# A two-layer encoder on one core: weight differences placed later in the queues, and block products in twos and threes behind every second up tile

## The chip, the cores and the metric

The kernel runs on one core of a Trainium2 chip. The metric is the device time of one execution in microseconds (us); lower is better. PE is the matrix engine (PEld its weight loads), DVE the vector engine, ACT the scalar engine, POOL and SP two further engines; here SP only issues the transfers of weights.

## The reference

Two layers, each an attention and Fourier mixer followed by a convolutional feed-forward block, on 272 tokens (16 of them dropped at the end) of 2048 channels. The change concerns the feed-forward block (D_FF = 5632):

```python
h2 = _rmsnorm(h_stream, norm_ffn[i])
up = h2 @ w_up[i]
u_gate = _dwconv3_centred(up[..., :D_FF], w_conv[i], b_conv[i])
u_val = up[..., D_FF:]
h_stream = h_stream + (jax.nn.silu(u_gate) * u_val) @ w_down[i]
```

All data are float32.

## The kernel before

**Chunks.** Every weight matrix is cut into chunks of 128 x 1024 float32 values (512 KB; four tiles of 128 rows by 256 columns). `order` lists all products of the kernel with their chunks, in the order in which PE takes them; `group` walks that list. A chunk passes through three engines: SP loads it into one of four `raw` buffers (`load_raw`), ACT rounds it to a high half `wh` (L230), DVE subtracts that from `raw` to get a low half `wl` (L233). `wh` and `wl` have three buffers each. `advance` and `pump` issue the halves two chunks ahead of the one that PE works on. PE multiplies high by high, high by low and low by high part of the data: for a gate group (`ug`, 258 or 272 columns wide) 24 matmuls per chunk (L304 to L306). In layer 1 a value group (`uv`) has both data parts side by side and takes 16 matmuls per chunk, 8 of them 512 wide (L300, L301).

**The up tiles.** Gate group `ug` i (4 chunks) and value group `uv` i (4 chunks) give 256 hidden channels. After a gate group comes its evacuation: for each half of 128 channels `u` (DVE, L1105), `cv` (ACT, L1107), two convolution steps on `cv` (DVE, L1109 and L1110), silu (ACT, L1111) and a product with `rstdB` (DVE, L1112).

**The block products.** The first 32 of the 44 tiles of the hidden channels of layer 1 do not go through an ordinary `w_down` product. They are taken in pairs of tiles, and seven products of blocks (`PRODUCTS`) replace eight; the data side of each is a combination `sx`, rounded to `cb` (L1017, L1018), and the weight side is a block of `w_down` or a difference of blocks. There are two sets of 16 tiles, so two sets of 7 x 8 = 56 products. Each is one chunk with 6 matmuls of 512 columns on PE (`block_`, L1046, `ps_x`); `gather` adds the result of 8 of them to `C4` (L1030). The first set is mixed into the 64 up chunks of the second 16 tiles, the second set into the 48 up chunks of the last 12. Where a product goes is decided in the loop around L170: `at` counts up chunks, `done` the products placed.

**The weight differences.** The four differences that each of the 16 pairs (`q`) needs are made during the feed-forward block of layer 0 by `weight_sums`, a generator that `step` advances (one call after every two of a chunk's eight pairs of tile and half, so four calls per up or down chunk). A block is loaded into `b0` to `b3` by a transfer that ACT issues (L977). Ahead of it ACT copies one column of the current `wh` into the buffer (L976), which ties the transfer to that place. DVE subtracts (L980), and ACT issues the store to `ts` in device memory (L982). The numbers in `yield 9` are calls of `step` until the generator goes on.

**What sets the order.** Each engine takes its queue in order. The framework's scheduler arranges the queue from the order of the code, the dependencies and its own estimates; buffers are reused when their last reader is through.

Of the kernel before, what the change touches and what calls it, by code (L numbers as in the profile page):

```python
# [10 lines left out]
F32 = mybir.dt.float32  # L11
F32R = mybir.dt.float32r
AF = mybir.ActivationFunctionType
ALU = mybir.AluOpType
AX = mybir.AxisListType

P = 128
D = 2048
# [17 lines left out]
NPR = sum(FF_SPLIT[-1][:2]) // 2  # L36
# [84 lines left out]
def encoder_kernel(ctx, tc, xT, params, consts, bmat, w_in, w_abr, w_four, w_f64, w_out, w_up, w_down, w_blk, outT):  # L121
    nc = tc.nc
    dram = ctx.enter_context(tc.tile_pool(name="dram", bufs=1, space=bass.MemoryType.DRAM))
    tsum = [[dram.tile([P, D // 2], F32, name=f"ts{q}_{e}") for e in range(4)] for q in range(NPR)]
# [7 lines left out]
    for l in range(DEPTH):  # L132
        def g(w, mg, k0, k1):
            return [(w[l, mg, c], CW) for c in range(k0 // CW, k1 // CW)]
        if l == 0:
            f01 = [g(w_in, IN_F + i, 0, KT) for i in range(2)]
            order.append(((l, "f01"), [ch for pr in zip(*f01) for ch in pr]))
        for i in range(2 if l == 0 else 0, 4):
            order.append(((l, "f", i), g(w_in, IN_F + i, 0, KT)))
        order.append(((l, "k", 0), g(w_in, IN_K, 0, KT)))  # L140
        order.append(((l, "v", 0), g(w_in, IN_V, 0, KT)))
        for i in range(4):
            order.append(((l, "q", i), g(w_in, IN_Q + i, 0, KT)))
        for half in range(2):
            for kind, j in BRANCH_ORDER[half]:
                w, off, n = {"ga": (w_in, IN_GA, KT), "gf": (w_in, IN_GF, KT), "s": (w_four, 0, 8), "a": (w_abr, 0, 8)}[kind]
                order.append(((l, kind, j), g(w, off + j, 0, n)))
            for mg in range(8):
                order.append(((l, "o", half, mg), g(w_out, mg, 8 * half, 8 * half + 8)))
        k0 = 0  # L150
        for c, n in enumerate(FF_SPLIT[l]):
            ups = []
            for i in range(k0 // MG, (k0 + n) // MG):
                ups.append(((l, "ug", i), g(w_up, i, 0, KT)))
                ups.append(((l, "uv", i), g(w_up, FT // MG + i, 0, KT)))
            if l == DEPTH - 1 and c:
                xs_, q0 = [], (k0 - FF_SPLIT[l][c - 1]) // 2
                for p, _ in PRODUCTS:
                    for q in range(FF_SPLIT[l][c - 1] // 2):
                        src = {1: w_blk[2 * (q0 + q), 0], 2: w_blk[2 * (q0 + q) + 1, 0], 3: w_blk[2 * (q0 + q) + 1, 1],  # L160
                               5: tsum[q0 + q][0], 7: tsum[q0 + q][1], 6: tsum[q0 + q][2], 4: tsum[q0 + q][3]}[p]
                        xs_.append((src.rearrange("p (c m) -> p c m", c=CW), (c - 1, p, q)))
                slots = sum(len(chs) for _, chs in ups)
                at = done = 0
                for u, (key, chs) in enumerate(ups):
                    mixed = []
                    for ch in chs:
                        mixed.append(ch)
                        at += 1
                        while done < len(xs_) and done * slots < at * len(xs_):  # L170
                            mixed.append(xs_[done])
                            done += 1
                    ups[u] = (key, mixed)
                assert done == len(xs_)
            order += ups
            if l < DEPTH - 1 or c == len(FF_SPLIT[l]) - 1:
                for mg in range(8):
                    order.append(((l, "d", c, mg), g(w_down, mg, k0, k0 + n)))
            k0 += n
# [3 lines left out]
    st = {"raw": 0, "fetch": 0, "next": 0, "grp": 0}  # L183
# [13 lines left out]
    def advance(upto):  # L197
        while st["raw"] < min(upto + RAW, len(chunks)):
            load_raw(st["raw"])
            st["raw"] += 1  # L200
        while st["fetch"] < min(upto, len(chunks)):
            i = st["fetch"]
            if i in folded:
                todo.append((i, lambda i=i: fold_w(i)))
            todo.append((i, lambda i=i: split_w(i, 0, CW)))
            st["fetch"] += 1
# [14 lines left out]
    def split_w(i, a, b, eng=None):  # L221
        if i not in splits:
            h = wp.tile([P, CW, MG * P], F32R, tag="wh", name=f"wh{i}")
            lo = wp.tile([P, CW * MG * P + 64], F32R, tag="wl", name=f"wl{i}")
            o = wl_at[i]
            splits[i] = h, lo[:, o:o + CW * MG * P].rearrange("p (c m) -> p c m", c=CW)
        h, lo = splits[i]
        r = raws[i]
        if eng is None:
            nc.scalar.copy(h[:, a:b], r[:, a:b])  # L230
        else:
            eng.tensor_copy(h[:, a:b], r[:, a:b])
        nc.vector.tensor_tensor(lo[:, a:b], r[:, a:b], h[:, a:b].bitcast(F32), op=ALU.subtract)  # L233
        if b == CW:
            del raws[i]
# [112 lines left out]
    def first_groups(pss):  # L348
# [17 lines left out]
        for i, c0, c1, ks in ((0, 0, 1, (0,)), (0, 1, 2, (1,)), (1, 0, 2, ()), (0, 2, 4, (2, 3)), (1, 2, 4, ())):  # L366
            for k in ks:
                norm_split(k, P_NM)
            split_w(i, c0, c1, nc.vector if (i, c0) == (0, 0) else None)
# [56 lines left out]
    small = ctx.enter_context(tc.tile_pool(name="small", bufs=4))  # L426
# [92 lines left out]
    for l in range(DEPTH):  # L519
# [7 lines left out]
        with tc.tile_pool(name=f"mix{l}", bufs=1) as mp:  # L527
# [394 lines left out]
            for half in range(2):  # L922
                mH = mL = None
                for kind, i in BRANCH_ORDER[half]:
# [19 lines left out]
                    else:  # L944
# [6 lines left out]
                        for m in range(MG):  # L951
                            k = 2 * j + m
                            t_, h_ = tha[i][:, m, lo:T], mH[:, k, lo:T]
# [13 lines left out]
        with tc.tile_pool(name=f"ffn{l}", bufs=1) as fp:  # L967
# [2 lines left out]

            def weight_sums():
                tt = nc.vector.tensor_tensor
                for q in range(NPR):
                    b = [fp.tile([P, D // 2], F32, tag=f"b{e}", name=f"b{e}") for e in range(4)]
                    for e, sums in ((0, ()), (1, ((0, 1, 0, 0),)), (3, ((1, 3, 1, 1), (3, 3, 0, 2))), (2, ((2, 2, 3, 3),))):
                        nc.scalar.copy(b[e][:, 0:1], st["cur"][:, 0, 0:1].bitcast(F32))  # L976
                        nc.scalar.dma_start(b[e], w_blk[2 * q + e // 2, e % 2])  # L977
                        yield 9
                        for o, x, y, to in sums:
                            tt(b[o], b[x], b[y], op=ALU.subtract)  # L980
                            yield 2
                            nc.scalar.dma_start(tsum[q][to], b[o])  # L982
                        yield 3

            sets, prods = [], {"have": {}}
            if last:
# [79 lines left out]
            if l == DEPTH - 2:  # L1066
                behindhand.append([24, weight_sums()])
# [142 lines left out]
```

## Time and profile before

| | |
|---|---|
| runs, median (lowest to highest of 3) | 2525.16 us (2524.92 to 2531.62) |
| the profiled execution's own time | 2528.11 us |
| its span, first to last instruction | 2526.0 us |
| mean granted PE clock | 0.999 |
| PE / PEld / DVE / ACT busy | 2511.2 / 2441.2 / 1852.2 / 1276.4 us |
| DMA | 557.63 MB, 221 GB/s on average |

The span is divided as follows: layer 0 up to about 530 us its mixer, 530 to 1230 its feed-forward block, and layer 1 after that; the block products run from about 1980 to 2450 us. The busy time of a matmul in the trace is longer than the distance to the next one, because matmuls overlap; the distance from one start to the next is read from the timeline.

### The profile page before, as it was taken

To read this page: it belongs to the slowest core of one execution; us is meant where nothing else is said; L and a number is where in the kernel's file an instruction comes from. 1 tells how busy PE (TensorE), PEld (TensorE's weight loads), DVE (VectorE), ACT (ScalarE), POOL (GpSimd) and SP (SyncE) were. 2 spreads that over 40 slices of the span, in tenths; PEclk is the share of its full clock that TensorE was granted. 3 is DMA by queue.
4 is the path that set the end of the run, shared out by engine and by line. 5 is a ranking of instruction groups with operands and counts; after the bars stand their busy time and mean duration, and the time that the engine had idled before them with its cause. 6 is when DMAs were issued, how large, how long until landed. Compare 5 with 4: busy or idle time off the path is not lost.

```text
span 2526.0 us, 47879 instructions
## 1 busy us (share of the span) xinstructions
PE 2511.2 (99%) x19404; PEld 2441.2 (97%) x19404; DVE 1852.2 (73%) x2851; ACT 1276.4 (51%) x1857; POOL 18.3 (1%) x37
## 2 busy tenths in 40 slices
PE   9999999999999999999999999999999999999999
PEld 9999999999999999999999999999999989988888
DVE  7687867776776556676556887677766788879985
ACT  6455544554444334444444564445644565556653
POOL 0000000000000000000000000000000000000000
PEclk9999999999999999999999999999999999999999
DMA  7545666568888887787554555666656677778875
GB/s 240 166 157 161 194 185 190 189 225 283 286 282 281 277 292 266 270 288 266 183 179 151 175 157 188 196 201 200 188 189 192 217 243 247 244 249 256 260 244 174
DMA packets 157501, 557.63 MB, mean 221 GB/s; under 512 B 18144, under 2 KB 22112, under 8 KB 157280
## 3 DMA queue, kind: packets, MB, share of 16 engines
q1 hardware_dynamic: 134480, 482.54, 59.5%
q10 hardware_dynamic: 22800, 72.04, 8.1%
q8 instruction: 152, 2.49, 0.4%
q14 instruction: 69, 0.57, 0.1%
HBM read 516.07 MB, written 35.65 MB: 218 GB/s over the span
## 4 chain that ended last, share of the span: by engine, by line
PE 95%; DVE 2%; DMA 1%; ACT 1%; issue 1%; ACTq 0%; SPq 0%; DVEq 0%
PE ps_ug L306 6%; PE ps_ug L304 6%; PE ps_uv L300 6%; PE ps_ug L305 6%; PE ps_x L1046 6%; PE ps_d L306 4%; PE ps_d L304 4%; PE ps_d L305 4%; PE ps_uv L301 3%; PE ps_uv L306 3%; PE ps_uv L304 3%; PE ps_uv L305 3%; PE ps_o L304 2%; PE ps_o L306 2%; PE ps_o L305 2%; PE ps_gf L304 2%
## 5 line engine op out<-in xcount | busy, mean ns | idle before, releaser
L233 DVE TENSOR_TENSOR wl<-raw,wh 128x1024 fp32r<-128x1024 f32 (+1 forms) x883 | 1073.8, 1220 | 442.5 <-ACT wh L230 438.2
L230 ACT CAST wh<-raw 128x1024 fp32r<-128x1024 f32 (+1 forms) x882 | 920.9, 1046 | 853.6 <-PE ps_ug L305 171.4
L306 PE MATMUL ps_ug<-xHL,wl 128*128 128x272 f32 (+1 forms) x1408 | 397.6, 282 | 2.7 <-DVE wl L233 2.7
L304 PE MATMUL ps_ug<-xHL,wh 128*128 128x272 f32 (+1 forms) x1408 | 399.1, 283 | 0.0
L305 PE MATMUL ps_ug<-xHL,wh 128*128 128x272 f32 (+1 forms) x1408 | 397.1, 282 | 0.0
L306 PEld LDWEIGHTS ps_ug<-xHL,wl 128*128 128x128 f32 x1408 | 264.5, 188 | 3.1 <-DVE wl L233 3.1
L305 PEld LDWEIGHTS ps_ug<-xHL,wh 128*128 128x128 f32 x1408 | 264.8, 188 | 2.2
L304 PEld LDWEIGHTS ps_ug<-xHL,wh 128*128 128x128 f32 x1408 | 264.3, 188 | 2.7
L300 PE MATMUL ps_uv<-xHL,wh 128*128 128x512 f32 x704 | 247.7, 392 | 0.0
L306 PE MATMUL ps_d<-gHL,wl 128*128 128x272 f32 (+1 forms) x728 | 208.3, 286 | 2.5 <-DVE wl L233 2.5
L304 PE MATMUL ps_d<-gHL,wh 128*128 128x272 f32 (+1 forms) x728 | 208.8, 287 | 0.0
L305 PE MATMUL ps_d<-gHL,wh 128*128 128x272 f32 (+1 forms) x728 | 207.4, 285 | 0.0
L304 PE MATMUL ps_uv<-xHL,wh 128*128 128x272 f32 x704 | 201.3, 286 | 0.0
L306 PE MATMUL ps_uv<-xHL,wl 128*128 128x272 f32 x704 | 200.7, 285 | 0.0
L305 PE MATMUL ps_uv<-xHL,wh 128*128 128x272 f32 x704 | 199.9, 284 | 0.0
L301 PE MATMUL ps_uv<-xHL,wl 128*128 128x256 f32 x704 | 198.3, 282 | 0.0
L300 PEld LDWEIGHTS ps_uv<-xHL,wh 128*128 128x128 f32 x704 | 132.0, 188 | 28.6
L1046 PE MATMUL ps_x<-wh,cb 128*128 128x512 f32 x448 | 156.6, 393 | 0.0
L304 PE MATMUL ps_ga<-xHL,wh 128*128 128x272 f32 (+1 forms) x512 | 147.0, 287 | 0.0
L304 PE MATMUL ps_gf<-xHL,wh 128*128 128x272 f32 (+1 forms) x512 | 145.8, 285 | 0.1
L304 PE MATMUL ps_o<-mH,wh 128*128 128x272 f32 (+1 forms) x512 | 144.6, 282 | 0.0
L306 PE MATMUL ps_ga<-xHL,wl 128*128 128x272 f32 (+1 forms) x512 | 144.6, 282 | 0.0
(306 smaller groups left out, 5979.8 us busy)
## 6 DMA issues: line engine op xcount, KB each, us to landing
raw<-in_w_up SPq DMA_DIRECT2D x352, 512.0 KB, 4.4
raw<-in_w_in SPq DMA_DIRECT2D x206, 512.0 KB, 3.6
raw<-in_w_down SPq DMA_DIRECT2D x112, 512.0 KB, 4.3
raw<-in_w_out SPq DMA_DIRECT2D x64, 512.0 KB, 3.9
b<-in_w_blk ACTq DMA_DIRECT2D x64, 512.0 KB, 5.0
ts<-b ACTq DMA_DIRECT2D x64, 512.0 KB, 3.6
raw<-ts SPq DMA_DIRECT2D x64, 512.0 KB, 4.5
raw<-in_w_blk SPq DMA_DIRECT2D x48, 512.0 KB, 4.4
```

Source lines behind the costliest of these rows:

```text
L230: nc.scalar.copy(h[:, a:b], r[:, a:b])
L233: nc.vector.tensor_tensor(lo[:, a:b], r[:, a:b], h[:, a:b].bitcast(F32), op=ALU.subtract)
L300: nc.tensor.matmul(o2, h[:, c, sl], ab, start=kt == 0, stop=False)
L301: nc.tensor.matmul(o, lo[:, c, sl], ab[:, 0, :], start=False, stop=kt == nk - 1)
L304: nc.tensor.matmul(o, h[:, c, sl], a, start=kt == 0, stop=False)
L305: nc.tensor.matmul(o, h[:, c, sl], b, start=False, stop=False)
L306: nc.tensor.matmul(o, lo[:, c, sl], a, start=False, stop=kt == nk - 1)
L1046: nc.tensor.matmul(ps[e], cb[:, s_, q - q4], w, start=q == 0 and a == 0, stop=q == n - 1 and a == 2)
```

## The change

```diff
-                        while done < len(xs_) and done * slots < at * len(xs_):
+                        while done < len(xs_) and at % 2 == 0 and done * slots < at * len(xs_):
...
             o = wl_at[i]
+            st["new"] = h
...
             def weight_sums():
                 tt = nc.vector.tensor_tensor
-                for q in range(NPR):
-                    b = [fp.tile([P, D // 2], F32, tag=f"b{e}", name=f"b{e}") for e in range(4)]
+                b, due = {}, []
+                for q in range(NPR + 1):
                     for e, sums in ((0, ()), (1, ((0, 1, 0, 0),)), (3, ((1, 3, 1, 1), (3, 3, 0, 2))), (2, ((2, 2, 3, 3),))):
-                        nc.scalar.copy(b[e][:, 0:1], st["cur"][:, 0, 0:1].bitcast(F32))
-                        nc.scalar.dma_start(b[e], w_blk[2 * q + e // 2, e % 2])
-                        yield 9
-                        for o, x, y, to in sums:
-                            tt(b[o], b[x], b[y], op=ALU.subtract)
-                            yield 2
-                            nc.scalar.dma_start(tsum[q][to], b[o])
-                        yield 3
+                        if q < NPR:
+                            t_ = fp.tile([P, D // 2], F32, tag=f"b{e}", name=f"b{e}")
+                            nc.scalar.copy(t_[:, 0:1], st["cur"][:, 0, 0:1].bitcast(F32))
+                            nc.scalar.dma_start(t_, w_blk[2 * q + e // 2, e % 2])
+                        yield 5
+                        if due:
+                            one = small.tile([P, 32], F32, tag="one", name="one", bufs=2)[:, 0:1]
+                            nc.scalar.activation(one, st["new"][:, 0, 0:1].bitcast(F32), AF.Identity, bias=1.0, scale=0.0)
+                        for o, x, y, to in due:
+                            nc.vector.scalar_tensor_tensor(o, x, one, y, op0=ALU.mult, op1=ALU.subtract)
+                            yield 3
+                            nc.scalar.dma_start(to, o)
+                        if q == NPR:
+                            return
+                        b[e] = t_
+                        yield 7 - 3 * min(len(due), 2)
+                        due = [(b[o], b[x], b[y], tsum[q][to]) for o, x, y, to in sums]
```

A difference is now issued after the next block's load instead of after its own block's. It is written as `x * one - y`, and `one` is a column of ones that ACT computes from the newest `wh`, so the difference cannot stand ahead of that cast. The tile `one` takes 2 x 128 bytes per partition in the pool `small`; all tiles of the layer's inner pools move by 256 bytes, those allocated earlier stay.

ACT at the first load into `b1`, before. Names carry the chunk's number (`wh176` is the high half of chunk 176) and a counter:

```order
L230 CAST wh176_7020<-raw176_6859 128x1024
L976 COPY b1_7007<-wh176_7020 128x1
L977 DMA b1_7007<-in_w_blk 128x1024
L230 CAST wh177_7050<-raw177_6893 128x1024
L1129 CAST gHL_6785<-cv_6930 128x272
```

DVE at the difference that reads it, before:

```order
L233 TENSOR_TENSOR wl177_7051<-raw177_6893,wh177_7050 128x1024
L1127 TENSOR_TENSOR cv_6930<-cv_6930,ps_0_uv_0_0_6944 128x272
L980 TENSOR_TENSOR b0_7006<-b1_7007,b0_7006 128x1024
L1130 TENSOR_TENSOR gHL_6785<-cv_6930,gHL_6785 128x272
L1127 TENSOR_TENSOR cv_6938<-cv_6938,ps_0_uv_0_1_6945 128x272
L233 TENSOR_TENSOR wl178_7089<-raw178_6946,wh178_7088 128x1024
```

ACT at the same load now:

```order
L231 CAST wh176_7017<-raw176_6859 128x1024
L979 COPY b1_7107<-wh176_7017 128x1
L980 DMA b1_7107<-in_w_blk 128x1024
L231 CAST wh177_7047<-raw177_6893 128x1024
L1139 CAST gHL_6785<-cv_6930 128x272
```

DVE at the difference that reads it now:

```order
L234 TENSOR_TENSOR wl182_7230<-raw182_7077,wh182_7229 128x1024
L1122 TENSOR_TENSOR cv_7205<-cv_7205,rstdB_141 128x272
L1119 SCALAR_TENSOR_TENSOR cv_7213<-u_7211,prm_134,cv_7213 128x271
L986 SCALAR_TENSOR_TENSOR b0_7006<-b1_7107,one_7259,b0_7006 128x1024
L1120 SCALAR_TENSOR_TENSOR cv_7213<-u_7211,prm_134,cv_7213 128x271
L234 TENSOR_TENSOR wl183_7263<-raw183_7110,wh183_7262 128x1024
```

The load stays behind cast 176; the difference moved from behind low half 177 to behind low half 182. Over all 64 differences the distance in chunks from the cast ahead of the last load that it needs to the low half ahead of the difference was 1 (53 times) or 2 (11 times), and is now 5 (5 times), 6 (47 times) or 7 (12 times). The loads begin at the same chunk; each group of four takes 12 chunks instead of 14.

SP's loads where the first set of products begins, before (`in_w_up` is an up chunk, `in_w_blk` a block product's):

```order
L190 DMA raw664_23967<-in_w_up 128x1024
L190 DMA raw665_23997<-in_w_blk 128x1024
L190 DMA raw666_24045<-in_w_up 128x1024
L190 DMA raw667_24067<-in_w_blk 128x1024
L190 DMA raw668_24089<-in_w_up 128x1024
L190 DMA raw669_24111<-in_w_blk 128x1024
L190 DMA raw670_24144<-in_w_up 128x1024
L190 DMA raw671_24180<-in_w_blk 128x1024
```

And now:

```order
L190 DMA raw664_24063<-in_w_up 128x1024
L190 DMA raw665_24093<-in_w_up 128x1024
L190 DMA raw666_24141<-in_w_blk 128x1024
L190 DMA raw667_24163<-in_w_blk 128x1024
L190 DMA raw668_24185<-in_w_up 128x1024
L190 DMA raw669_24207<-in_w_up 128x1024
L190 DMA raw670_24240<-in_w_blk 128x1024
L190 DMA raw671_24276<-in_w_blk 128x1024
```

Up chunks and products alternated; now two follow two. Behind the fourth up chunk of a gate group this puts two products between the group's last matmul and the next group. DVE there, before (the gate group's evacuation falls between the low halves of chunks 672 and 673):

```order
L233 TENSOR_TENSOR wl672_24287<-raw672_24194,wh672_24286 128x1024
L1105 TENSOR_TENSOR u_24320<-ps_1_ug_8_0_24142,rstdB_141 128x258
L1105 TENSOR_TENSOR u_24328<-ps_1_ug_8_1_24143,rstdB_141 128x258
L1109 SCALAR_TENSOR_TENSOR cv_24322<-u_24320,prm_134,cv_24322 128x256
L1110 SCALAR_TENSOR_TENSOR cv_24322<-u_24320,prm_134,cv_24322 128x255
L233 TENSOR_TENSOR wl673_24314<-raw673_24224,wh673_24313 128x1024
```

And now:

```order
L234 TENSOR_TENSOR wl671_24371<-raw671_24276,wh671_24370 128x1024
L1115 TENSOR_TENSOR u_24416<-ps_1_ug_8_0_24238,rstdB_141 128x258
L1115 TENSOR_TENSOR u_24424<-ps_1_ug_8_1_24239,rstdB_141 128x258
L1119 SCALAR_TENSOR_TENSOR cv_24418<-u_24416,prm_134,cv_24418 128x256
L1120 SCALAR_TENSOR_TENSOR cv_24418<-u_24416,prm_134,cv_24418 128x255
L234 TENSOR_TENSOR wl672_24398<-raw672_24306,wh672_24397 128x1024
```

Chunk 672 is the first value chunk in both orders. Its low half stood ahead of the evacuation and now stands behind four of its operations.

## The prediction

> **What bounds the kernel now.** I read the page's busy line first, then the waits of PE, DVE and ACT, then the timeline around PE's longest wait, and last PE's pace around the block products.
>
> ```profile
> PE 2511.2 (99%) x19404; PEld 2441.2 (97%) x19404; DVE 1852.2 (73%) x2851; ACT 1276.4 (51%) x1857; POOL 18.3 (1%) x37
> ```
>
> PE is busy for 2511.2 of 2526.0 us. A change can win only from the 14.8 us in which it idles, or from the pace at which matmuls follow each other. The waits (waiter, who ended it, total us, times, longest) say where part of the idle time comes from:
>
> ```profile
> PE ps_ug L306 <- DVE wl L233: 2.7, 2, 1.7
> PE ps_d L306 <- DVE wl L233: 2.5, 1, 2.5
> DVE b L980 <- DMA b<-in_w_blk: 69.3, 44, 4.9
> ACT wh L230 <- DVE b L980: 30.2, 8, 6.6
> ```
>
> In 44 of its 64 weight differences DVE stands in front of a DMA that has not landed, 69.3 us in all. DVE takes its queue in order, so a low half `wl` behind such a difference is late too; three times that reaches PE, for 5.2 us. The third, in the timeline:
>
> ```profile
> 1176.38 0.34 ACTq L977 DMA_DIRECT2D b<-in_w_blk  x1
> ...
> 1184.03 0.28 PE L305 MATMUL ps_d<-gHL,wh 128*128 128x272 f32 x1
> ...
> 1184.35 1.23 DVE L980 TENSOR_TENSOR b<-b,b 128x1024 f32<-128x1024 f32 x1 [4.86 <-DMA b<-in_w_blk]
> 1185.49 1.22 DVE L233 TENSOR_TENSOR wl<-raw,wh 128x1024 fp32r<-128x1024 f32 x1
> ...
> 1186.77 0.39 PE L306 MATMUL ps_d<-gHL,wl 128*128 128x272 f32 x1 [2.46 <-DVE wl L233]
> ```
>
> The block is requested at 1176.38, DVE waits 4.86 us for it, the difference takes 1.23, the `wl` behind it 1.22, and PE stands for 2.46. From one start to the next that is 2.74 us. Right behind it, two windows (bounds, length, busy of PE, PEld, DVE, ACT, POOL, granted clock, DMA):
>
> ```profile
> 1187.60:1191.00 3.40, 3.40 (x17) 3.40 (x16) 2.76 (x6) 1.64 (x4) 0.00 (x0) 0.50 0.92 294
> 1191.00:1194.40 3.40, 3.40 (x30) 3.40 (x29) 2.56 (x3) 1.43 (x4) 0.00 (x0) 1.00 0.96 343
> ```
>
> For 3.4 us the granted clock is 0.50 and 17 matmuls fall into a stretch that holds 30 afterwards: 3.4 x 0.5 = 1.7 us more. I put this on the stall, since nothing else idles PE there. At full clock the spacing is 0.11 to 0.12 us, so the 2.74 above lost 2.62, some 0.16 more than the wait says; the same at the two others makes it 5.7 us in all.
>
> **Step 1, the weight differences (layer 0).** Removed: 64 `tt` on DVE. Added: 64 differences in the three-operand form and 48 one-column activations on ACT (one for each load after which something is due: 3 for each of 16 `q`). Moved: each difference. Today it stands 1 or 2 chunks behind the cast after which its block was requested; in the changed order 5 to 7 (47 times 6). An up chunk in layer 0 is 24 matmuls of 0.11 to 0.12, about 2.8 us, and 5 chunks are 14 us.
>
> ```profile
> L976 ACT COPY b<-wh x64: 173/191/194, 532.9 to 1191.0; 128x1 f32<-128x1 f32 x64
> L980 DVE TENSOR_TENSOR b<-b,b x64: 1216/1226/1228, 547.4 to 1195.4; 128x1024 f32<-128x1024 f32 x64
> DMA to landing us min/median/max: 2.6/4.6/7.9
> ```
>
> The slowest landing is 7.9 us, so the wait on the DMA should vanish from DVE: minus 5.7 us for PE, and minus 1.7 for the clock. Costs: ACT's 48 one-column activations, priced like the one-column copy (0.191), are 9 us over some 560, beside an engine that is half idle: nothing. The three-operand form with a column as scalar takes 0.48 for 256 columns in the rows further down, the two-operand form 0.42 for 258; so 1.23 becomes about 1.29, 64 x 0.06 = 4 us of DVE, covered by the 69 us that it no longer waits. The gate `one` stands on ACT right behind the cast that DVE's preceding `wl` needed anyway; where it stands one cast later, DVE loses up to a cast (1.05), which the distance to PE covers. Loads come every 12 chunks in fours, not every 14; with 4 stores each that is 20 transfers for 12 chunks instead of 22 for 14, 6% more traffic, and the weight loads have four buffers of lead. ACT's load into `b1` now follows the store out of the old `b1` by two chunks (over 5 us, median landing 4.6): ACT may wait a little, PE not. Bounds for step 1: 0 (the waits only change place) to -7.4; I take -7.4, since 14 us are well beyond 7.9.
>
> On the clock the Trainium skill (TensorE: Matmul & The Clock Gate, section HAM oscillation — how this bites in real kernels) warns of gaps over about 3.4 us. The gap here is 2.74 and the half clock came all the same; by that rule the 1.7 would have another cause and stay, and the end would come 1.7 us later than I forecast.
>
> **Step 2, the blocks in twos and threes (layer 1).** No work is added; blocks only change place. I write U for an up chunk, X for a block. Before, an X stands behind nearly every U. Now the first set of products has 24 pairs and 8 single X, the second 16 pairs and 8 triples, always behind two U. PE's pace, from the first matmuls of chunks:
>
> ```profile
> 1918.83 0.28 PE L304 MATMUL ps_ug<-xHL,wh 128*128 128x258 f32 x1
> 1921.61 0.28 PE L304 MATMUL ps_ug<-xHL,wh 128*128 128x258 f32 x1
> ...
> 2049.99 0.39 PE L1046 MATMUL ps_x<-wh,cb 128*128 128x512 f32 x1
> 2051.38 0.28 PE L304 MATMUL ps_ug<-xHL,wh 128*128 128x258 f32 x1
> 2054.22 0.39 PE L1046 MATMUL ps_x<-wh,cb 128*128 128x512 f32 x1
> ...
> 2064.10 0.39 PE L300 MATMUL ps_uv<-xHL,wh 128*128 128x512 f32 x1
> 2066.87 0.40 PE L1046 MATMUL ps_x<-wh,cb 128*128 128x512 f32 x1
> ```
>
> A gate chunk behind another takes 2.78 (1918.83 to 1921.61), behind an X 2.84. The chain prices X:
>
> ```profile
> 2394.90 1.39 PE ps_x L1046 x6
> 2403.31 2.74 PE ps_x L1046 x12
> ```
>
> Alone 1.39, two in a row 2.74, so a second one costs 1.35 to 1.37. A value chunk behind X takes 2.77, no dearer than a gate chunk; I count nothing there. The first set has 8 rounds of 8 U. In each, two gate chunks now follow a gate chunk (0.06 each), and three X come to stand behind an X (1.39 less 1.35, 0.04 each): 0.24, 1.9 in all. The second set: 12 gate chunks x 0.06 and 24 more X behind an X x 0.04, 1.7; but in the first set one gate chunk per round that followed a value chunk now follows an X, which I price at the same 0.06 against it: -0.5. Together -3.1; bounds 0 and -3.6.
>
> Against it stands DVE. A chunk's cast needs the `wh` buffer of the chunk three places back. For a U behind two X that buffer comes free when PE enters the first X; the `wl` is needed 2 X later and one 512-wide matmul (0.23) more: 2.74 + 0.23 = 2.97 us. Cast (1.04) and subtraction (1.23) take 2.3 if nothing else stands between. At the end of a gate group the evacuation does. The same evacuation in the trace, before one X:
>
> ```profile
> 2030.06 0.42 DVE L1105 TENSOR_TENSOR u<-ps_ug,rstdB 128x258 f32<-128x258 f32 x1
> ...
> 2030.48 0.39 PE L1046 MATMUL ps_x<-wh,cb 128*128 128x512 f32 x1
> ...
> 2030.52 0.60 ACT L1107 ACTIVATE cv<-u,prm 128x256 f32<-128x256 f32 x1 [1.63 <-DVE u L1105]
> 2030.68 0.43 DVE L1105 TENSOR_TENSOR u<-ps_ug,rstdB 128x258 f32<-128x258 f32 x1 [0.20 <-PE ps_ug L306]
> ...
> 2031.02 1.04 ACT L230 CAST wh<-raw 128x1024 fp32r<-128x1024 f32 x1
> 2031.15 0.48 DVE L1109 SCALAR_TENSOR_TENSOR cv<-u,prm,cv 128x256 f32<-128x256 f32 x1
> ...
> 2031.67 0.48 DVE L1110 SCALAR_TENSOR_TENSOR cv<-u,prm,cv 128x255 f32<-128x255 f32 x1
> ...
> 2032.09 1.23 DVE L233 TENSOR_TENSOR wl<-raw,wh 128x1024 fp32r<-128x1024 f32 x1
> ```
>
> From X's first matmul (2030.48) to the end of the subtraction (2033.32) is 2.84, and the changed order has the same rows there (`u u cv cv wl672`): 0.13 us to spare, at 11 group ends. Where one more operation of 512 columns stands between (0.69), PE waits: one place with all of it (some 0.5), two where it replaces a 0.48 (0.1 each); the U behind a triple at a gate group's end has one X less (two places, some 0.25 each), one at a value group's end 0.25. Sum +1.5 us. Today's order has such a place too:
>
> ```profile
> 2298.43 2.35 DVE L233 TENSOR_TENSOR wl<-raw,wh 128x1024 fp32r<-128x1024 f32 x2
> ...
> 2299.31 0.40 PE L300 MATMUL ps_uv<-xHL,wh 128*128 128x512 f32 x1
> 2299.71 0.38 PE L301 MATMUL ps_uv<-xHL,wl 128*128 128x256 f32 x1
> ```
>
> The low half starts 0.40 after the high one instead of 0.23: 0.17 us lost behind a pair of X. So +1.5 has bounds 0 (every margin holds) and 56 x 0.17 = 9.5 (each of 48 U and 8 X behind two X like this one).
>
> **Step 3, the byte places.** `one` shifts every tile of the two inner pools by 256 bytes. Rows of `mH` lie 1280 bytes apart, so they stand at 0, 256, 512 and 768 modulo 1024 in turn, and
>
> ```profile
> L304 PE MATMUL ps_o<-mH,wh x512: 278/282/287, 318.6 to 1803.7; 128*128 128x272 f32 x86, 128*128 128x258 f32 x85
> ```
>
> its fastest and slowest matmul lie 9 ns apart with two widths in it. A step of 256 bytes changes no pace there: 0. If it did, by 3 ns on some 5000 matmuls that read the moved tiles (those of `ps_o`, `ps_a`, `ps_d` and `ps_s`), it would be 15 us either way.
>
> **Sum.** -7.4 - 3.1 + 1.5 = -9.0: span 2526.0 to 2517.0, own time 2528.11 to 2519.1. The median of the runs, 2525.16, lies 2.95 under the profiled execution. If that run merely had more of the stalls that go, the changed kernel ends at 2519.1; if the 2.95 lie elsewhere, at 2516.2. Two of the three runs agree within 0.24 us, which waits of varying length would hardly do, so I lean to the second: 2517.3, 0.31% under 2525.16. About 0.3% (7.6 us) is what a measurement of this kernel tells from no change, so the forecast stands on that line.
>
> **Rivals.**
> A, slower: DVE becomes the bound of layer 1's products.
>
> ```profile
> 2262.00:2452.00 190.00, 190.00 (x1147) 169.14 (x1147) 165.12 (x213) 117.27 (x145) 0.00 (x0) 1.00 0.81 257
> ```
>
> In the second set DVE is busy for 165 of 190 us, and its order puts evacuations ahead of the low halves wanted behind two X. For it: the 0.13 us margin; against: where nothing stands between, 2.97 - 2.3 leaves 0.6. To end 7.6 us above 2525.16 it must eat the 7.9 us won and 7.6 more, 15.5 over the 56 places behind two X: from 0.28 us at each on top of the 1.5, more than the worst place today lost. Time 2533 and up; chance 0.05. Half of it, some 0.14 at each, gives 2525: no change, 0.07.
>
> B, the weight differences keep stalling PE: ACT, in order, waits for the store out of `b1` or for the difference before it stores, and the casts behind it are late (today ACT waits 30.2 us for `b`, up to 6.6). Against it: ACT is no longer behind a DVE that waits for a landing. The 7.4 stay: 2517.3 + 7.4 = 2524.7, no change; chance 0.08.
>
> C, grouping wins nothing: the gate chunk behind an X is longer for what ACT and DVE write meanwhile, not for the X. Then -3.1 falls away: 2520.4, no change; chance 0.10. The Trainium skill (the same page, section Wait — 56ns, not 53.3ns?) has each warm matmul start N / 2.4 + 2.5 ns after the last, whatever stood before; that would give C's time. The rows above speak against it: the same 24 matmuls took 2.78 and 2.84.
>
> D, the byte places matter after all: up to 15 us either way, so 2502 to 2532; chance 0.03, one third each.
>
> E, more is won: every margin behind two X holds (+1.5 becomes 0) and the pace gives its bound (-3.6): 2514.2 by the second reading of the median; chance 0.07.
>
> **How the numbers follow.** The forecast itself has 0.60: 2515.5 to 2520 (the two readings of the median, the rounding of step 2). It lies on the line, so I give 0.40 of it to faster and 0.20 to no change. Faster: 0.40 + 0.07 + 0.01 = 0.48. No change: 0.20 + 0.07 + 0.08 + 0.10 + 0.01 = 0.46. Slower: 0.05 + 0.01 = 0.06. The range takes in B and C above and E below: 2512.5 to 2525.5; it leaves out A's far side and D.
>
> **What will show it.** Step 1: DVE's waits for the DMA of `b` near 0 instead of 69.3, no wait of PE for `wl` between 530 and 1200 us, the granted clock 1.00 throughout, the last difference some 75 us earlier (behind low half 368 instead of 395, 27 chunks of 2.8). If B holds, ACT waits for a store or for `b` and PE still waits for `wl`. Step 2: half as many pieces of X in the chain, most with 12 or 18 matmuls; gate chunks of 2.78 behind a gate chunk; PE waits for `wl` behind pairs and triples of 1 to 2 us in all, at the ends of gate groups. The forecast is wrong on the slow side if that wait exceeds 5 us.

## The result and the profile after

The changed kernel takes 2517.93 us (median of 7 runs, 2517.44 to 2519.97) against 2525.16 us before (2523.85 to 2532.36); the ratio is 0.9966, 95% interval 0.9954 to 0.9978. Forecast were 2517.3 us (range 2512.5 to 2525.5) and a ratio of 0.9969. The profiled execution took 2518.45 us with a span of 2516.0, 9.7 and 10.0 us less than before; the sum said 9.0.

The page's busy line after, the waits of PE (both the first two rows) and what is left of them:

```profile
PE 2505.6 (100%) x19404; PEld 2436.0 (97%) x19404; DVE 1853.7 (74%) x2851; ACT 1280.8 (51%) x1905; POOL 18.3 (1%) x37
PE ps_f L362 <- ACT wh L231: 3.8, 4, 1.4
PE ps_s L341 <- DVE wl L234: 1.1, 2, 0.8
```

The two rows of before, `ps_ug` 2.7 and `ps_d` 2.5 behind DVE's `wl`, are gone. What is left stands at the start of the program and in the mixer of layer 1. The rows on the tiles `b` after (times min/median/max in ns, then what the engines that write them waited for: the first row is ACT ahead of its one-column copy, the second DVE ahead of a difference):

```profile
L986 DVE SCALAR_TENSOR_TENSOR b<-b,one,b x64: 1274/1277/1286, 563.3 to 1108.1; 128x1024 f32<-128x1024 f32 x64
...
  DVE cv L1122: 3.8, 5
  ACT one L984: 2.9, 5
...
DMA to landing us min/median/max: 3.6/5.3/9.5
```

No wait for a DMA is among them any more, though the landings, loads and stores together, became slower (median 5.3 instead of 4.6, longest 9.5 instead of 7.9). DVE now reaches a difference 16.7 us or more after the request of the last block that it needs. The gate `one` costs DVE 2.9 us in 5 waits, the three-operand form takes 1.277 us instead of 1.226. The last difference starts at 1108.1 instead of 1195.4, 87 us earlier where some 75 were forecast. A window over the whole stretch shows PE busy all the time at full clock, where 662 us before held 5.1 us of idling:

```profile
523.00:1200.00 677.00, 677.00 (x5540) 676.92 (x5539) 469.88 (x594) 315.32 (x485) 0.85 (x1) 1.00 0.81 279
```

Where the 10 us are from can be read at the first matmuls of the stages, in the timeline of before and of after: the feed-forward block of layer 0 begins with the first `ps_ug`, the next layer with `ps_f`, its feed-forward block with `ps_ug` again.

```profile
522.51 0.29 PE L304 MATMUL ps_ug<-xHL,wh 128*128 128x272 f32 x1
...
1305.56 0.29 PE L304 MATMUL ps_f<-xHL,wh 128*128 128x272 f32 x1
...
1804.05 0.28 PE L304 MATMUL ps_ug<-xHL,wh 128*128 128x258 f32 x1
```

```profile
523.86 0.29 PE L305 MATMUL ps_ug<-xHL,wh 128*128 128x272 f32 x1
...
1299.09 0.29 PE L305 MATMUL ps_f<-xHL,wh 128*128 128x272 f32 x1
...
1796.51 0.28 PE L305 MATMUL ps_ug<-xHL,wh 128*128 128x258 f32 x1
```

Layer 0's block fell from 783.05 to 775.23 us (-7.8), layer 1's mixer from 498.49 to 497.42 (-1.1, not touched by the change), layer 1's block from 721.96 to 719.5 (-2.4, to the spans' ends). The start grew by 1.35, with the waits of `ps_f` for ACT there (3.8 us instead of 2.5).

### The profile page after: what moved, and what is told of

It reads as the page before. It is cut to its first block, busy times and chain, and to the rows that moved or that the text cites. A ratio compares the mean times of both kernels' runs of the same rounds, so it can differ in the third digit from the quotient of the medians.

```text
span 2516.0 us, 47967 instructions
## 1 busy us (share of the span) xinstructions
PE 2505.6 (100%) x19404; PEld 2436.0 (97%) x19404; DVE 1853.7 (74%) x2851; ACT 1280.8 (51%) x1905; POOL 18.3 (1%) x37
## 4 chain that ended last, share of the span: by engine, by line
PE 97%; DVE 1%; ACT 1%; issue 0%; DMA 0%; SPq 0%; ACTq 0%; DVEq 0%
PE ps_ug L305 7%; PE ps_ug L307 7%; PE ps_ug L306 7%; PE ps_uv L301 6%; PE ps_x L1056 6%; PE ps_d L307 4%; PE ps_d L305 4%; PE ps_d L306 4%; PE ps_uv L307 3%; PE ps_uv L305 3%; PE ps_uv L306 3%; PE ps_uv L302 3%; PE ps_o L305 2%; PE ps_o L307 2%; PE ps_o L306 2%; PE ps_ga L305 2%
## 5 line engine op out<-in xcount | busy, mean ns | idle before, releaser
L1056 PE MATMUL ps_x<-wh,cb 128*128 128x512 f32 x448 | 148.1, 391 | 0.0
```

The source lines that it names most:

```text
L1056: nc.tensor.matmul(ps[e], cb[:, s_, q - q4], w, start=q == 0 and a == 0, stop=q == n - 1 and a == 2)
```

## The experiments

Stage lengths are read as above from each run's timeline. Between runs without waits for a DMA they repeat to 0.01 us in layer 0's block, so a single profile tells more here than the times, which before scatter by 16 us. The medians are of 12 runs for `a_only` and `b_only`, 10 for `plain_tt` and `pad256`, 7 to 9 for the others, and 2 for `early`.

| run | median us | ratio to before, 95% | layer 0's block | layer 1's block |
|---|---|---|---|---|
| before | 2525.16 | | 783.0 | 722.0 |
| changed | 2517.93 | 0.9966, 0.9954 to 0.9978 | 775.2 | 719.5 |
| a_only | 2519.89 | 0.9971, 0.9960 to 0.9983 | 775.2 | 722.4 |
| b_only | 2521.93 | 0.9981, 0.9969 to 0.9994 | 778.8 | 718.9 |
| plain_tt | 2521.82 | 0.9983, 0.9971 to 0.9995 | 780.9 | 718.9 |
| early | 2549.37 | 1.0085, 1.0058 to 1.0111 | 804.9 | 722.0 |
| mid4 | 2518.91 | 0.9966, 0.9954 to 0.9978 | 775.2 | 720.6 |
| end4 | 2518.46 | 0.9962, 0.9949 to 0.9975 | 775.2 | 722.2 |
| odd | 2519.85 | 0.9969, 0.9959 to 0.9980 | 775.2 | 721.5 |
| pad256 | 2526.36 | 1.0002, 0.9988 to 1.0017 | 782.2 | 722.0 |
| pad64 | 2535.66 | 1.0028, 1.0007 to 1.0048 | 784.0 | 720.4 |
| pad128 | 2537.47 | 1.0030, 1.0019 to 1.0042 | 797.8 | 722.6 |

Each ratio goes against runs of the kernel before on the same chip; beside the 2525.16 of the first two rows those medians were 2526.91, 2527.58 and 2529.58 us, so that medians of different rows do not always compare.

**The two parts alone.** `a_only` has the late differences, `b_only` the grouping; each is the changed kernel without the other part's lines.

```diff
a_only: -  while done < len(xs_) and at % 2 == 0 and done * slots < at * len(xs_):
a_only: +  while done < len(xs_) and done * slots < at * len(xs_):
b_only: before, with the condition at % 2 == 0 added
```

> Only the late weight differences; the products stand one at a time as before. My theory (the stalls of layer 0 and their half clock are all of this part): span 2526.0 less 7.8, about 2518 (layer 0's feed-forward block 775 us instead of 783), time about 2519.5, ratio 0.9975 to 0.998; DVE waits under 5 us for blocks, no wait of PE for the low half there, clock 1.00. The rival that the two parts need each other, or that the 256 bytes do it: layer 0's block stays near 783, ratio 0.999 or more.

> Only the products in twos and threes; the weight differences as before. My theory: layer 0's block as before (780 to 785 us, stalls for the low half, longest 2 to 3 us), layer 1's feed-forward block 2.4 us shorter (719.5 instead of 722.0), with 2 to 3 us of waits for the low half behind pairs in it; ratio 0.998 to 1.000. The rival that grouping wins nothing: layer 1's block 722 or more, ratio 1.000.

`a_only` came out at 2519.89 us with layer 0's block at 775.24, the same to 0.01 us as with both parts. `b_only` left layer 0's stalls (its waits list PE behind `wl` in `ps_ug`, 1.5 us in 3 waits; the block of 778.8 lies a little under the 780 expected) and shortened layer 1's block by 3.1 us, more than the 2.4 expected. So each part does its work without the other. With both, layer 1's block is 0.6 us longer than in `b_only`: 0.25 up to the last matmul, the rest at the program's end. The waits of `a_only` hold no row of layer 0's block:

```profile
PE ps_f L362 <- ACT wh L231: 2.9, 3, 1.7
PE ps_s L341 <- DVE wl L234: 1.4, 3, 0.5
```

The runs tell one more thing. The 35 runs of before on this chip go from 2520.13 to 2536.04, the 12 of `b_only` from 2516.26 to 2530.64, the 12 of `a_only` from 2519.18 to 2521.64. No kernel with the late differences spreads over more than 3.9 us. In the profiles without them the stalls of layer 0 stand at other chunks and have other lengths each time (its block takes 778.8 to 797.8 us in five of them), as they hang on when blocks land; with the late differences no wait of PE there depends on it.

**Late in the code, but not in the queue.** `plain_tt` issues the differences at the late places, as plain subtractions and without `one`.

```diff
-  one = small.tile(...); nc.scalar.activation(one, st["new"][:, 0, 0:1].bitcast(F32), ...)
-  nc.vector.scalar_tensor_tensor(o, x, one, y, op0=ALU.mult, op1=ALU.subtract)
+  tt(o, x, y, op=ALU.subtract)
```

> The changed kernel with the differences issued at the same late places of the code, but as two-operand subtractions without the gate on the newest cast (the 256 bytes are kept by an unused tile). In the built order every difference then stands 1 chunk behind its load again instead of 5 to 7. If the place in DVE's queue is the cause: DVE waits 60 to 130 us for the blocks again, PE waits for the low half, layer 0's block 781 to 795 us, time 2521 to 2535. If the later place in the code, the shorter cycle of 12 chunks or the three-operand form is the cause: as the changed kernel, layer 0's block 775 us and 2518.

In the trace 58 of the 64 differences stand 1 chunk behind their load and 6 stand 2, and the waits of DVE for blocks are back (from the rows on `b`, and the waits of PE):

```profile
  DMA b<-in_w_blk: 53.0, 42
```

```profile
PE ps_uv L307 <- DVE wl L234: 1.8, 3, 0.8
...
PE ps_d L307 <- DVE wl L234: 0.7, 1, 0.7
```

Layer 0's block takes 780.9 us, 5.6 more than with the gate (781 to 795 were expected), and the runs spread over 9.0 us again. DVE waits less than expected (53 us, not 60 to 130); the longest landing was 6.9 us in that profile. So neither the later place in the code nor the shorter cycle brings the gain: `plain_tt` has both. It lacks the gate and the three-operand form together. The form without the gate was not run, but it only takes DVE 0.05 us more for each difference, and what came back without the two is the waits for blocks. So it is the place in DVE's queue that brings the gain, and the dependency on the newest cast is what holds a difference there.

**Sooner in the code.** `early` is the kernel before with the difference 4 calls after its load.

```diff
-  yield 9
+  yield 4
```

> The kernel before with the differences issued 4 calls after their load instead of 9, so that DVE reaches them sooner: double the suspected cost. My theory: DVE waits more than 69 us for the blocks (100 to 200), PE's waits for the low half in layer 0 rise to 10 to 40 us, and half-clock windows of 3.4 us come behind the longest gaps (2.5 us and more). Rival (DVE's wait is not what reaches PE): layer 0's block stays at 778 to 784 us; rival on the clock (a half-clock window comes at random): none, or one away from any gap.

It took 2549.37 us, layer 0's block 804.9. The edit did not do what was meant. DVE reached a difference 4.15 us after the request of its last block (median of 64), and 4.21 before: the differences stood right behind their loads already. What the smaller number changed is how densely the loads come, one every 7.1 us instead of 10.4. The waits of PE, the matmuls behind four of its gaps, and windows at these gaps (granted clock third from the end):

```profile
PE ps_uv L306 <- DVE wl L233: 13.5, 8, 4.0
PE ps_ug L306 <- DVE wl L233: 4.3, 3, 1.9
```

```profile
697.61 0.40 PE L306 MATMUL ps_ug<-xHL,wl 128*128 128x272 f32 x1 [1.89 <-DVE wl L233]
...
717.27 0.39 PE L306 MATMUL ps_uv<-xHL,wl 128*128 128x272 f32 x1 [3.13 <-DVE wl L233]
...
752.56 0.39 PE L306 MATMUL ps_ug<-xHL,wl 128*128 128x272 f32 x1 [1.93 <-DVE wl L233]
...
822.40 0.60 PE L306 MATMUL ps_uv<-xHL,wl 128*128 128x272 f32 x1 [4.04 <-DVE wl L233]
```

```profile
698.71:702.12 3.41, 3.41 (x18) 3.41 (x17) 2.52 (x4) 2.45 (x5) 0.00 (x0) 0.50 0.84 223
...
717.30:721.00 3.70, 3.70 (x30) 3.70 (x31) 2.54 (x3) 1.17 (x2) 0.00 (x0) 1.00 0.91 312
753.33:756.74 3.41, 3.41 (x17) 3.41 (x17) 3.41 (x5) 2.49 (x4) 0.00 (x0) 0.50 0.88 316
...
821.59:828.42 6.83, 6.02 (x26) 6.02 (x27) 3.38 (x4) 1.99 (x3) 0.00 (x0) 0.50 0.89 311
```

Ahead of each of PE's five longest waits DVE stood 2.4 to 4.2 us in front of a difference whose block had not landed, so waits of DVE turned into waits of PE, as my theory had it; DVE's own wait, at 89 us, rose less than the 100 to 200 expected. The half clock comes at gaps, so not at random, but their length alone does not decide: after the wait that ended at 717.27 (3.1 us) the clock stayed full, after those that ended at 697.61 and 752.56 (1.9 us each) it halved for 3.41 us, and at the longest (4.0 us) for 6.83.

**Where the pairs stand.** Three other places for the products, all with the late differences.

```diff
mid4: +  ... at % 4 == 2 and done * slots < (at + 2) * len(xs_):
end4: +  ... at % 4 == 0 and done * slots < at * len(xs_):
odd:  +  ... at % 2 == 1 and done * slots < (at + 1) * len(xs_):
```

> The changed kernel with all block products of a group of four up chunks behind the second of them: three or four in a row in the first set, four or five in the second, none at a group's end. Half as many changes between up chunk and product again, and no evacuation between a run of products and the next low half. My theory (pace at the changes, waits only where an evacuation stands there): layer 1's feed-forward block 715 to 717.5 us instead of 719.5, waits of PE for the low half there under 1.5 us, time 2514 to 2516.5. The rival that runs of products are bound by DVE (1.22 us of subtraction for 1.37 us of PE, so any other operation tips it): several us of waits, block 721 or more, time 2519 or more.

> The same number of products in a row as in the run with all of them behind the second up chunk, but behind the fourth, where the group's evacuation falls. The pace gains as much. My theory: waits of PE for the low half of 4 to 9 us at the gate groups' ends (about 14 of them, 0.2 to 0.5 us each, on the third or fourth product), layer 1's block 718 to 723 us, time 2517 to 2521, worse than behind the second chunk. Rival (the place does not matter): the same time as behind the second chunk.

> The changed kernel with pairs and triples behind the first and third up chunk of a group instead of the second and fourth: as many changes, none at a group's end, but the evacuation's second half falls on the pair behind the first chunk. My theory: pace as in the changed kernel, waits moved from the group's end to the chunk behind that pair, layer 1's block 718 to 721 us, time 2516.5 to 2519.5. If the group's end alone is the trouble: waits under 0.5 us and 717.5 us.

The main waits of PE's weight loads for `wl` in layer 1's block, changed kernel first, then `mid4`, `end4` and `odd` (most of such a wait is covered by the matmul still running):

```profile
PEld ps_uv L302 <- DVE wl L234: 2.3, 9, 0.4
...
PEld ps_x L1056 <- DVE wl L234: 0.3, 1, 0.3
```

```profile
PEld ps_x L1056 <- DVE wl L234: 4.1, 10, 0.9
...
PEld ps_uv L302 <- DVE wl L234: 1.1, 4, 0.5
```

```profile
PEld ps_x L1056 <- DVE wl L234: 8.1, 23, 1.2
```

```profile
PEld ps_uv L302 <- DVE wl L234: 1.3, 3, 0.6
...
PEld ps_x L1056 <- DVE wl L234: 0.5, 1, 0.5
```

`mid4` missed: layer 1's block takes 720.6 us, not 715 to 717.5. Two things that I had not priced eat what fewer changes give. The third product in a row takes 1.424 us on average instead of 1.36 (28 of them), the fifth 1.416: rows of four and five run into DVE, as the rival said, though by less. And where no product stands at a group's end, a gate chunk follows a value chunk directly, which costs 2.81 instead of 2.77 (21 times instead of 8). `end4` has the waits expected (8.1 us on the weight loads) and the block expected, 722.2; the times of both differ by less than their spread. `odd` lies half a microsecond beyond its range: its chunks behind products and second products are some 2 us longer than their like (four of them by 0.3 to 0.5), and 21 gate chunks follow a value chunk there too. Twos and threes behind every second up chunk gave the shortest block of the four; by their times (ratios 0.9962 to 0.9969) the four cannot be told apart.

**The byte places.** An unused tile in the pool `small` of the kernel before:

```diff
 small = ctx.enter_context(tc.tile_pool(name="small", bufs=4))
+small.tile([P, 64], F32, name="place", bufs=1)   # pad256; 16 columns in pad64, 32 in pad128
```

> The kernel before with an unused tile of 256 bytes in the pool small, so that all tiles of the inner pools stand where they stand in the changed kernel. If these byte places do not matter: PE's pace in every stage as before, layer 1's mixer 497 to 499 us, time 2524 to 2532, ratio 0.999 to 1.001. If they do: the pace of the matmuls that read the moved tiles differs by some ns, the two mixers and the down products by several us.

> The kernel before with an unused tile of 64 bytes, so that the tiles of the inner pools move by 64 bytes, where the changed kernel moves them by 256 and the run with 256 unused bytes showed no change. If a tile's place counts modulo 256 bytes: the pace of matmuls that read moved tiles (ps_o, ps_a, ps_d, ps_s) changes by 1 to 5 ns for some groups, several us in the mixers or down products (1500 matmuls of ps_o x 3 ns is 4.5 us), in either direction. If places do not count at all: every stage that has no wait for a DMA as before (layer 1's blocks 257.8 and 210.1 us, down part 72.6 us).

> The same with 128 unused bytes: half of the move that the changed kernel makes. If places count modulo 128 bytes, as with 256: no group's pace differs by 1 ns. If they count modulo 256: a change of pace of the size that the move by 64 bytes shows, several us in the mixers or down products.

The rows of the output projection in the groups of `pad256`, `pad64` and `pad128` (busy us, mean ns):

```profile
L305 PE MATMUL ps_o<-mL,wh 128*128 128x272 f32 (+1 forms) x512 | 143.3, 280 | 0.0
```

```profile
L305 PE MATMUL ps_o<-mL,wh 128*128 128x272 f32 (+1 forms) x512 | 146.2, 286 | 0.0
```

```profile
L305 PE MATMUL ps_o<-mL,wh 128*128 128x272 f32 (+1 forms) x512 | 145.1, 283 | 0.0
```

Before, this row read 143.3, 280, as in `pad256`. By starts, the matmuls of 272 columns that read `mL` stand 120 ns apart before and in `pad256`, 126 in `pad64` and 123 in `pad128`; with 256 bytes no large group's median moved by 1 ns. 64 and 128 bytes cost 0.28% and 0.30%, nearly all that the changed kernel wins. Not all of `pad128` is pace: its profile, of the slowest of its 8 runs (2547.08 us), has 8.8 us of waits for `wl` in layer 0's block, where before has 5.2, and two stretches of half clock.

Not every stage got slower. With 64 bytes layer 1's block is 1.6 us shorter than before (720.4), with the products in the same places. First matmuls of a product, a gate chunk and a product in `pad64`:

```profile
1994.48 0.40 PE L1047 MATMUL ps_x<-wh,cb 128*128 128x512 f32 x1
...
1995.88 0.28 PE L304 MATMUL ps_ug<-xHL,wh 128*128 128x258 f32 x1
...
1998.67 0.40 PE L1047 MATMUL ps_x<-wh,cb 128*128 128x512 f32 x1
```

A gate chunk behind a product takes 2.79 there, where it took 2.85 before, and still 2.77 behind a gate chunk; a second product in a row takes 1.40, no less than a first. So what a change between up chunk and product costs depends on where the tiles stand. By these lengths grouping would win some 0.5 us there (an estimate: 0.02 at each of 28 gate chunks, nothing on the products), not 3.

## Why the prediction was right, point by point

**The weight differences, -7.4.** Measured -7.8 in layer 0's block. The block's matmuls are the same before and after, so their starts can be compared one by one: the three waits cost 1.25, 2.01 and 2.72 us, the half clock 1.60, and two slow matmuls at 987 us, too short for the list of waits, 0.23. The forecast's terms were 5.7 for the waits (5.98 measured, as one more matmul is 0.11 late behind each) and 1.7 for the clock. The rows carried it: a landing of 7.9 us at most against a distance of 14 us. `plain_tt` shows that the distance is the cause. Rival B (the stalls stay on ACT's side) is out: `a_only` has none.

**The clock, -1.7 within it.** It went with the stalls. That the 2.74 us gap "caused" the half clock is only half the story. In `early` the half clock began at 698.71, 753.33 and 821.59, which lie 16.0 and 20.0 times 3.413 us apart, and lasted one or two such stretches: a fixed grid. Laid over that grid the twelve profiles part cleanly, from the first record of full clock to the last matmul. In seven stretches of 3.413 us at full clock PE idles for 1.74 us or more, as the trace draws it, and half clock follows every one; in all the others it idles for 1.73 at most, and half clock follows none. The 3.1 us of `early` fell into two stretches, 1.64 and 1.49; its waits of 1.9 fell into one each. So the grid decides which gap is paid for. The Trainium skill (TensorE: Matmul & The Clock Gate, section What's actually happening) states free-running windows of 3413 ns, and these distances agree; its rule of gaps over about 3.4 us, weighed in the prediction, does not hold as a threshold here.

**The pace, -3.1.** From the first `ps_ug` to the end of the last product, layer 1 went from 649.35 to 646.55 us, -2.8. The chunks behind two products were longer than their usual length by 0.84 us together (28 value chunks at 2.817 instead of 2.792 on average, 8 third products at 1.383 instead of 1.366). The order before had such a chunk too, the value chunk at 2299.31 that the prediction shows, which is 0.26 longer than its like. So the pace itself gave -3.4, between the forecast and the bound named. First matmuls after, of two products, two gate chunks and a product:

```profile
1980.77 0.39 PE L1056 MATMUL ps_x<-wh,cb 128*128 128x512 f32 x1
...
1983.53 0.28 PE L305 MATMUL ps_ug<-xHL,wh 128*128 128x258 f32 x1
...
1986.37 0.28 PE L305 MATMUL ps_ug<-xHL,wh 128*128 128x258 f32 x1
...
1989.14 0.39 PE L1056 MATMUL ps_x<-wh,cb 128*128 128x512 f32 x1
```

The two products take 2.76, the gate chunk behind them 2.84, the next 2.77. That the sum came so near is in part luck, as its terms missed in opposite directions. The gate chunks gave -2.1, not -1.2: those behind a product took 2.85 before, and the eight that followed a value chunk took 2.82 there already, so that moving them behind a product cost 0.02 each and not 0.06. The products gave -1.0, not -1.9: a second one takes 0.02 less than a first on average, not 0.04, since a first one behind a value chunk takes only 1.38. The value chunks, counted as nothing, gave -0.3. Rival C (grouping wins nothing) fell: after, a gate chunk took 2.773 behind a gate chunk and 2.836 behind a product. In `pad64` it would have come near, so what grouping wins hangs on the byte places too; why was not tried. The price of nothing for what stood before, which the Trainium skill (TensorE: Matmul & The Clock Gate, section Wait — 56ns, not 53.3ns?) would give, has no support in these rows.

**The waits behind pairs, +1.5.** This term was too large by a factor of nearly two: 0.84, or 0.58 without the 0.26 that before had already. Its places were right in part. The one with a whole extra operation, priced at 0.5, is the longest value chunk (2.999 at 2152.09, 0.21 lost), and the two behind a triple at a gate group's end lost 0.10 each, not 0.25. The two where an operation is replaced and the one at a value group's end lost nothing. Of the places not priced, two ordinary gate groups' ends lost 0.15 and 0.16, one third product 0.12, and two chunks 0.06 and 0.07. The first of these group ends, in the timeline of after:

```profile
2021.14 0.39 PE L1056 MATMUL ps_x<-wh,cb 128*128 128x512 f32 x1
...
2021.84 1.04 ACT L231 CAST wh<-raw 128x1024 fp32r<-128x1024 f32 x1
2021.97 0.49 DVE L1119 SCALAR_TENSOR_TENSOR cv<-u,prm,cv 128x256 f32<-128x256 f32 x1 [0.20 <-ACT cv L1117]
...
2022.49 0.48 DVE L1120 SCALAR_TENSOR_TENSOR cv<-u,prm,cv 128x255 f32<-128x255 f32 x1
...
2022.92 1.22 DVE L234 TENSOR_TENSOR wl<-raw,wh 128x1024 fp32r<-128x1024 f32 x1
...
2023.91 0.40 PE L301 MATMUL ps_uv<-xHL,wh 128*128 128x512 f32 x1
2024.20 0.39 PE L302 MATMUL ps_uv<-xHL,wl 128*128 128x256 f32 x1
```

From the first product (2021.14) to the end of the subtraction (2024.14) are 3.00 us, where 2.84 were worked out and 2.97 needed: the matmul with the low half starts 0.29 us behind the one with the high half instead of 0.23. DVE waits 0.20 us for `cv` in this evacuation (the row at 2021.97), which is more than the 0.13 to spare. The margin is as thin as it looked, and a miss costs one or two tenths of a microsecond, since PE starts as soon as the half is there. Nine of the 14 gate groups' ends lost 0.01 or less. Rival A, slower, needed 0.28 us at each of 56 places; the mean was 0.015.

**The byte places, 0.** Right, as `pad256` shows, and Rival D's bound of 15 us was not idle: 64 or 128 bytes cost some 7 us in the median, in `pad128` partly in stalls.

**The median.** Here the reason was wrong. I took the agreement of two runs as a sign that the profiled execution's extra 2.95 us lay outside the stalls. The 35 later runs of before show a spread of 16 us. The two readings gave 2516.2 and 2519.1; it became 2517.93, and the changed kernel's profiled execution lies only 0.5 us above its median. The forecast's closeness is in part luck. Both parts won more than forecast, layer 0's block 0.4 us and layer 1's 1.2 up to the last product, 1.6 together; the start, layer 1's mixer and the end of the program (+1.35, -1.1 and +0.4), on which the forecast had no term, took 0.6 of that back in the profile. And the median of before in the result, 2525.16, lies 1.8 to 4.4 us below those of its later runs.

One item has no explanation: with differences that stand late in the queue the program ends 3.8 us after its last matmul starts, without them 3.4, in every profile. The step lies in SP's closing sequence, where one wait ends 0.36 us behind the one before it instead of 0.06; why was not tried.

## What to carry to other kernels

On an engine that takes its queue in order, an operation that waits for a transfer delays everything behind it; look how far, in units of the work between them, the operation stands behind its transfer's issue, and make that longer than the longest landing, not the median. Issuing it later in the code need not do that where a scheduler arranges the queue; here a real dependency on something late did. If a change adds a small tile, check what it shifts: here 256 bytes were free and 64 cost 0.28%.

## What the runs showed that I had not expected

- A run-to-run spread of 16 us (0.6%) was itself the sign of waits for transfers on the way to PE; without them it was 2 to 4 us.
- The half clock follows a grid of 3.413 us: it came wherever PE, at full clock, idled 1.74 us or more within one stretch of the grid, and not where it idled less. So a stall of 1.9 us can cost 1.6 us more while one of 3.1 costs nothing more.
- Moving a matmul's data by 64 or 128 bytes changes its spacing (120 to 126 or 123 ns); by 256 bytes not. It also changes what a switch between two kinds of chunk costs (0.07 us to 0.02 for a gate chunk behind a product).
